# The set-up of an SSM's tables moved from beside the first FFN's down stage to beside its gate/up stage

## The chip, the cores and the metric

The kernel runs on one core of a Trainium2 chip. The metric is the device time of one execution in microseconds. The engines are named as in the profile: PE is TensorE (matmul), PEld its weight loads, DVE is VectorE, ACT is ScalarE, POOL is GpSimd, SP is SyncE. POOL, SP and ACT also issue DMAs.

## The reference, cut to what matters

One layer is computed for 1024 prompt tokens and 64 sample tokens together (1088 columns), all in float32:

```python
x = x + 0.5 * swiglu(rmsnorm(x), gate_a, up_a, down_a)      # first FFN: 1024 -> 2816 -> 1024
h = rmsnorm(x); q, k, v, u, g_attn, g_ssm = split(h @ w_in)
attn = windowed attention with sinks (q, k, v)
ssm  = glu(gelu(Re(C state_t) + D * u_t))                   # 32 groups, 64 states, 16 channels
x = x + (sigmoid(g_attn) * attn + sigmoid(g_ssm) * ssm) @ w_out
x = x + 0.5 * swiglu(rmsnorm(x), gate_b, up_b, down_b)      # second FFN, the same shapes
```

The SSM has a complex diagonal state per group: `abar = exp(lam * dt)`, `bbar = (abar - 1) / lam * b`, `h_t = abar * h_(t-1) + bbar * u_t`, `y_t = Re(c * h_t) + d * u_t`. The kernel evaluates it in chunks of eight tokens with tables that depend on the weights alone: powers of `abar` times `b` and `c`, the kernel of eight taps, and cosines and sines of the chunk's angle. Computing these tables is the set-up.

## The kernel before, in words

**Precision.** Every float32 operand of the large matmuls is split into a high part (rounded to fp32r by ACT) and a low part (the difference, by DVE), and each product is three matmuls.

**Stages of an FFN.** A start stage does two of 22 blocks of gate and up in the plain way. `g_stage` (L602) does the other 20, one unit each, by a Strassen scheme of seven products: per unit the steps P1, D (of the unit before), P6, P5, P27, each of several products of 12 matmuls, for two halves e of the columns. Weights come by SP's queue (L523), operands are split three steps ahead (`tasks`, L652 to L657), and the results are gathered by L705, L714, L721, L728 and L730; L732 writes the hidden block `hd` to DRAM from POOL's queue. Products X lie in PSUM banks of tags a and b (two buffers each), V and Y in tag d (three buffers). Then eight `d_unit`s (L779) read two or three hidden blocks and down weights back each, split them, and accumulate into x (L817), banks d and a. The first FFN's names end in a (psda, hida), the second's in b. The second FFN runs through the same `g_stage` and the same first seven `d_unit`s with nothing beside them.

**The side generator.** `run_units` runs the units' main generators one after another; each yield of a main is one tick (in `g_stage` one for six matmuls, 28 a unit, 560 in all; in a down unit of three blocks 36). `body` can attach a side generator: at each tick `rate` is added to an accumulator that starts at minus the lead, and for every full 1.0 the generator goes one step. The order of instructions on each engine is the order of these calls; the engines work in order, and waits between them are put in by the framework.

**The set-up** (`ssm_setup`, L897) is such a generator of 177 steps: loads of parameters on POOL's queue, some 24 steps on tiles of 128x32 (exponentials by a power on POOL, polynomials on DVE), and then eight blocks q of 19 steps on tiles of 128x512. A block transposes c (cT, L1072), makes S and C on DVE, transposes S (vl, L1092), forms k (L1100), makes C2 (L1110 to L1114), then the phases lo, ph, kk, kc (L1123 to L1136), the sines on ACT (L1138 to L1140), and writes each table to DRAM from POOL's queue (L1088 to L1147). The tables are read much later, in `ssm_core`. Small tiles come from a pool of five buffers (`s.sm`), large ones (weights, hidden blocks, operands, the parameter tile prm, ae, ssmin) from 43 buffers of one tag (`s.B`), PSUM banks by tag from `s.bank`: d 3, a 2, b 2, m 1. Before the change it is attached to `units[1]`, the first down unit, with rate 1.0 and lead 12.

Of the kernel before, what the change touches and what calls it, by code (L numbers as in the profile page):

```python
# [12 lines left out]
D = 1024  # L13
# [53 lines left out]
class Kern:  # L67
# [829 lines left out]
    def ssm_setup(s):  # L897
        nc, a = s.nc, s.a
# [2 lines left out]
        kpad = s.dr([16, NG, 256], "kpad")  # L901
        prm, ae, inp = s.B([128, 34, 32], "prm", F32), s.B([128, T], "ae", F32), s.B([128, 2, 512], "ssmin", F32)
        s.keep = s.small([128, 3, 32], "keep")
        free = list(range(34))

        def P():
            return prm[:, free.pop(0), :]
# [11 lines left out]
        def load_part(q):  # L919
            t = inp[:, q % 2, :]  # L920
            g0 = 4 * q
            for dst, hf, n in ((0, 0, "ssm_b_re"), (0, 1, "ssm_b_im"), (64, 0, "ssm_b_im"), (64, 1, "ssm_b_re")):
                nc.gpsimd.dma_start(t[hf * 64:(hf + 1) * 64, dst:dst + 64].rearrange("n (g c) -> n g c", g=4),
                                  a[n][0, g0:g0 + 4].rearrange("g n c -> n g c"))
            for dst, n in ((128, "ssm_c_re"), (192, "ssm_c_im"), (256, "ssm_c_im"), (320, "ssm_c_re")):
                nc.gpsimd.dma_start(t[0:64, dst:dst + 64], a[n][0, g0:g0 + 4].rearrange("g c n -> (g c) n"))
# [5 lines left out]
        for q in range(8):  # L932
            nc.gpsimd.dma_start(kpad[:, 4 * q:4 * q + 4, 0:128], z.rearrange("c (g x) -> c g x", g=4))
        yield
        ps = s.bank("b", "lamT")
        for i in range(2):
            nc.tensor.transpose(ps[:, i * 32:(i + 1) * 32], lam[:, i, :], s.id[:32, :32])
        lr, li, dt, mg, ang = P(), P(), P(), P(), P()
# [3 lines left out]
        e, c, p0 = P(), P(), P()  # L942
# [19 lines left out]
        def turns(x):  # L962

            k, kc, r = P(), P(), P()
            V.tensor_scalar(k, x, 1.0 / PI2, MAG, op0=OP.mult, op1=OP.add)
            V.tensor_scalar(kc, k, MAG, C14, op0=OP.subtract, op1=OP.mult)
            V.tensor_sub(r, x, kc)
            V.tensor_scalar(k, k, MAG, PI2 - C14, op0=OP.subtract, op1=OP.mult)
            return r, k

        r, k = turns(ang)
# [14 lines left out]
        V.scalar_tensor_tensor(sn, s2, 2.0, c2, op0=OP.mult, op1=OP.mult)  # L986
        V.tensor_mul(cs, s2, s2)
        yield
        t8, rhi, rlo = P(), P(), P()
        V.tensor_scalar(t8, ang, 8.0, None, op0=OP.mult)  # L990
        p8, q8 = turns(t8)
        yield
# [62 lines left out]
        V.tensor_scalar(AI, AI, -1.0, None, op0=OP.mult)  # L1055
        yield
        io = s.c1[:, C_IO:C_IO + 128]
        for q in range(8):
            g0 = 4 * q
            it = inp[:, q % 2, :]  # L1060
            gs = slice(g0, g0 + 4)

            def coef(x, lo, hi):
                n = hi - lo
                return x[:, lo:hi, gs].rearrange("p t g -> p g t").unsqueeze(3).to_broadcast([128, 4, n, 16])

            def chan(x, n):
                return x.rearrange("p (g c) -> p g c", g=4).unsqueeze(2).to_broadcast([128, 4, n, 16])

            pc = s.bank("b", f"cT{q}")  # L1070
            for i in range(2):
                nc.tensor.transpose(pc[:, i * 64:(i + 1) * 64], it[0:64, 128 + i * 128:256 + i * 128], s.id[:64, :64])  # L1072
            A.activation(it[:, 384:512], pc[:, 0:128], AF.Copy)
            bst, bsw, cc, csw = it[:, 0:64], it[:, 64:128], it[:, 384:448], it[:, 448:512]
            S, W = s.sm([128, 4, 8, 16], f"S{q}"), s.sm([128, 4, 8, 16], f"W{q}")
            V.tensor_mul(S, coef(ER, 0, 8), chan(bst, 8))
            yield
            V.tensor_mul(W, coef(EI, 0, 8), chan(bsw, 8))
            yield
            V.tensor_add(S, S, W)  # L1080
            yield
            C, W = s.sm([128, 4, 9, 16], f"C{q}"), s.sm([128, 4, 9, 16], f"W2{q}")
            V.tensor_mul(C, coef(AR, 0, 9), chan(cc, 9))
            yield
            V.tensor_mul(W, coef(AI, 0, 9), chan(csw, 9))
            yield
            V.tensor_add(C, C, W)
            nc.gpsimd.dma_start(s.tab1[gs, :, 192:320].rearrange("g p x -> p g x"), C[:, :, 1:9, :].rearrange("p g t c -> p g (t c)"))  # L1088
            yield
            pv = s.bank("b", f"vl{q}")  # L1090
            for g in range(4):
                nc.tensor.transpose(pv[:, g * 128:(g + 1) * 128], S[:, g].rearrange("p s c -> p (s c)"), s.id)  # L1092
            vl = s.sm([128, 4, 128], f"vls{q}")
            A.activation(vl, pv.rearrange("p (g x) -> p g x", g=4), AF.Copy)
            nc.gpsimd.dma_start(s.tab1[gs, :, 0:128].rearrange("g p x -> p g x"), vl)
            nc.gpsimd.dma_start(s.tab1[gs, :, 128:192].rearrange("g p x -> p g x"), vl[:, :, 0:64])
            yield
            pk = s.bank("b", f"k{q}")
            for g in range(4):
                nc.tensor.matmul(pk[:16, g * 128:(g + 1) * 128], S[:, g, 0, :], C[:, g, 0:8, :].rearrange("p t c -> p (t c)"), start=True, stop=True)  # L1100
            ks = s.sm([16, 4, 128], f"ks{q}")
            A.activation(ks, pk[:16].rearrange("p (g x) -> p g x", g=4), AF.Copy)
            dg = s.small([16, 4, 16], "dg", 2)
            V.tensor_mul(dg, s.id[0:16, 0:16].unsqueeze(1).to_broadcast([16, 4, 16]), dT[:, gs].unsqueeze(2).to_broadcast([16, 4, 16]))
            yield
            V.tensor_add(ks[:, :, 0:16], ks[:, :, 0:16], dg)
            nc.gpsimd.dma_start(kpad[:, gs, 128:256], ks)
            yield
            C2, W = s.sm([128, 4, 8, 16], f"D{q}"), s.sm([128, 4, 8, 16], f"W3{q}")
            V.tensor_mul(C2, coef(AI, 1, 9), chan(cc, 8))  # L1110
            yield
            V.tensor_mul(W, coef(AR, 1, 9), chan(csw, 8))
            yield
            V.tensor_sub(C2, C2, W)  # L1114
            nc.gpsimd.dma_start(s.tab2[gs, :, 0:128].rearrange("g p x -> p g x"), C2.rearrange("p g t c -> p g (t c)"))
            yield
            if q + 2 < 8:
                load_part(q + 2)
            ph, kk = s.sm([128, 4, 128], f"ph{q}"), s.sm([128, 4, 128], f"kk{q}")
            kc = s.sm([128, 4, 128], f"kc{q}")  # L1120
            iob = io.unsqueeze(1).to_broadcast([128, 4, 128])
            lo = s.sm([128, 4, 128], f"lo{q}")
            V.tensor_mul(ph, iob, rhi[:, gs].unsqueeze(2).to_broadcast([128, 4, 128]))  # L1123
            V.tensor_mul(lo, iob, rlo[:, gs].unsqueeze(2).to_broadcast([128, 4, 128]))
            yield
            V.tensor_add(kk, ph, lo)
            V.tensor_scalar(kk, kk, 1.0 / PI2, MAG, op0=OP.mult, op1=OP.add)
            yield
            V.tensor_scalar(kc, kk, MAG, C14, op0=OP.subtract, op1=OP.mult)
            V.tensor_scalar(kk, kk, MAG, PI2 - C14, op0=OP.subtract, op1=OP.mult)  # L1130
            yield
            V.tensor_sub(ph, ph, kc)
            V.tensor_sub(lo, lo, kk)
            yield
            V.tensor_add(ph, ph, lo)
            V.tensor_scalar(ph, ph, PIC, -PIC, op0=OP.min, op1=OP.max)  # L1136
            yield
            A.activation(kk, ph, AF.Sin, scale=0.5)  # L1138
            A.activation(kk, kk, AF.Square)
            A.activation(ph, ph, AF.Sin, scale=ns)  # L1140
            yield
            V.tensor_scalar(kk, kk, -2.0, 1.0, op0=OP.mult, op1=OP.add)
            nc.gpsimd.dma_start(s.tab3[gs, :, 0:128].rearrange("g p x -> p g x"), kk)
            nc.gpsimd.dma_start(s.tab3[gs, :, 128:256].rearrange("g p x -> p g x"), ph)
            yield
# [749 lines left out]
def at(u, before=None, after=None):  # L1895

    if before:
        main = u.main

        def run():  # L1900
            before()
            yield from main()
        u.main = run
    if after:
        u.end = after
    return u


def body(ctx, tc, a, o):
    s = Kern(ctx, tc, a, o)  # L1910
# [12 lines left out]
    def side(gen, rate, lead=0.0):  # L1923

        def f():
            s.drain_side()
            s.side, s.rate, s.acc = gen(), rate, -lead
            if lead:
                next(s.side)
        return f  # L1930

    units = s.ffn_units("a", ("f", 1))
    at(units[1], before=side(s.ssm_setup, 1.0, 12.0))

    def mix_begin():
        s.hready = 0
# [9 lines left out]
    q = [s.q_unit(f) for f in range(KC)]  # L1946
# [65 lines left out]
```

## Time and profile before

| | us |
|---|---|
| median of 3 runs (2352.77 to 2354.19) | 2353.74 |
| the profiled execution | 2351.03 |
| its span | 2349.3 |
| start, 0 to 90.4 | 90.4 |
| gate/up of the first FFN, 90.4 to 514.1 | 423.7 |
| down of the first FFN, units 1 to 7, 514.1 to 792.9 | 278.8 |
| down, unit 8 with the norm's sums, 792.9 to 831.8 | 38.9 |
| projections, attention, SSM, merge, start of the second FFN, 831.8 to 1645.6 | 813.8 |
| gate/up of the second FFN, 1645.6 to 2069.3 | 423.7 |
| down of the second FFN, units 1 to 7, 2069.3 to 2295.3 | 226.0 |
| last unit with the final norm, 2295.3 to 2349.3 | 54.0 |

The boundaries are read from the timeline of PE, by the tiles that its matmuls write. The windows view gives each engine's busy time between two times, the waits view who waited for whom. A matmul's length in the timeline overlaps the next one's; the distance between two starts is what it costs.

### The profile page before, as it was taken

The page shows a single profiled execution, that of the slowest core. Times are in us where ns is not written, and L with a number is a line of the kernel's source. Part 1 is how long each engine was busy: PE and PEld are TensorE (multiplying, and loading weights), DVE is VectorE, ACT ScalarE, POOL GpSimd, SP SyncE. Part 2 cuts the span into 40 slices and gives each one's busy share as a digit, 9 for nine tenths or more (in the row PEclk, how much of TensorE's full clock was granted, in tenths as well). Part 3 has the DMA queues.
Part 4 walks back from the last instruction along what each step waited for, and adds up shares of the span by engine and source line. Part 5 has one row for each costly group of instructions (what it writes and reads, how often), then busy time and mean ns, then how long its engine had stood idle before and what let it go on. Part 6 is the DMA issues. An engine that isn't in the chain of part 4 may idle for free. (4 is left out here: it accounts for less than half of the span.)

```text
span 2349.3 us, 39687 instructions
## 1 busy us (share of the span) xinstructions
PE 2275.0 (97%) x15910; PEld 2216.6 (94%) x15910; DVE 1404.2 (60%) x2961; ACT 853.0 (36%) x1919; POOL 264.3 (11%) x427
## 2 busy tenths in 40 slices
PE   7999999999889999999999999999999999999998
PEld 6999999998878998999998999989999999999997
DVE  7655555568888742446775666457555555575555
ACT  5333333331221341236666653223333333322113
POOL 2000000014333140002221100000000000000000
PEclk9999999999999999999999999999999999999999
DMA  6222222273443237740224164203222222362202
GB/s 197 79 73 83 83 75 64 83 255 108 140 138 106 73 131 215 238 107 28 69 75 111 45 231 136 73 5 140 79 83 66 73 83 83 126 256 72 86 10 77
DMA packets 234104, 250.04 MB, mean 106 GB/s; under 512 B 35056, under 2 KB 197024, under 8 KB 233888
## 3 DMA queue, kind: packets, MB, share of 16 engines
q1 hardware_dynamic: 218208, 205.42, 28.2%
q0 software_dynamic: 14272, 39.79, 4.8%
q8 instruction: 125, 2.05, 0.4%
q10 hardware_dynamic: 1440, 2.31, 0.3%
q14 instruction: 59, 0.48, 0.1%
HBM read 176.93 MB, written 74.60 MB: 107 GB/s over the span
## 5 line engine op out<-in xcount | busy, mean ns | idle before, releaser
L817 DVE SCALAR_TENSOR_TENSOR xr<-psdb,xr 128x384 f32<-128x384 f32 x168 | 87.9, 534 | 93.2 <-PE psdb L113 92.9
L817 DVE SCALAR_TENSOR_TENSOR xr<-psda,xr 128x384 f32<-128x384 f32 (+1 forms) x192 | 100.7, 532 | 33.5 <-PE psda L113 33.1
L1534 POOL TENSOR_SCALAR sm<-sm,sum 128x256 f32<-128x256 f32 x128 | 59.9, 487 | 312.3 <-DVE sum L1532 202.9
L113 PE MATMUL Ya<-b21h,a12a 128*128 128x272 f32 x320 | 67.1, 290 | 0.0
L113 PE MATMUL Xa<-t4h,a22a 128*128 128x272 f32 x320 | 67.1, 290 | 0.0
L113 PE MATMUL Yb<-b21h,a12b 128*128 128x272 f32 x320 | 67.1, 290 | 0.0
L113 PE MATMUL Xb<-t4h,a22b 128*128 128x272 f32 x320 | 67.1, 290 | 0.0
L113 PE MATMUL Vb<-b22h,s4b 128*128 128x272 f32 x320 | 67.1, 290 | 0.0
L113 PE MATMUL Va<-b22h,s4a 128*128 128x272 f32 x320 | 67.1, 290 | 0.0
L732 POOL DMA_DIRECT2D hd<-hidb x40 | 21.6, 540 | 403.0 <-DVE hidb L730 403.0
L732 POOL DMA_DIRECT2D hd<-hida x40 | 21.6, 540 | 403.0 <-DVE hida L730 403.0
L1518 ACT ACTIVATE sm<-sm,nm 128x256 f32<-128x256 f32 x128 | 63.3, 503 | 2.0 <-DVE nm L1505 1.9
L113 PE MATMUL Xa<-t2h,s2a 128*128 128x272 f32 x320 | 63.8, 290 | 0.0
L113 PE MATMUL Va<-t1h,s1a 128*128 128x272 f32 x320 | 63.8, 290 | 0.0
L113 PE MATMUL Xa<-t3h,s3a 128*128 128x272 f32 x320 | 63.8, 290 | 0.0
L113 PE MATMUL Xb<-t2h,s2b 128*128 128x272 f32 x320 | 63.8, 290 | 0.0
L113 PE MATMUL Xb<-t3h,s3b 128*128 128x272 f32 x320 | 63.8, 290 | 0.0
L113 PE MATMUL Vb<-t1h,s1b 128*128 128x272 f32 x320 | 63.8, 290 | 0.0
L113 PE MATMUL Xb<-b11h,a11b 128*128 128x272 f32 x320 | 63.8, 290 | 0.0
L113 PE MATMUL Xa<-b11h,a11a 128*128 128x272 f32 x320 | 63.8, 290 | 0.0
L104 ACT ACTIVATE hidhb<-rhidb 128x1088 fp32r<-128x1088 f32 x22 | 24.3, 1103 | 89.7 <-PE psdb L113 65.1
L113 PEld LDWEIGHTS Ya<-b21h,a12a 128*128 128x128 f32 x320 | 52.7, 188 | 0.0
(1455 smaller groups left out, 8498.9 us busy)
## 6 DMA issues: line engine op xcount, KB each, us to landing
xr<-xd SPq DMA_DIRECT2D x24, 544.0 KB, 6.0
rhida<-hd SPq DMA_DIRECT2D x22, 544.0 KB, 5.2
rhidb<-hd SPq DMA_DIRECT2D x22, 544.0 KB, 5.2
rdowna<-in_ffn_a_down_dram SPq DMA_DIRECT2D x22, 512.0 KB, 3.9
rdownb<-in_ffn_b_down_dram SPq DMA_DIRECT2D x22, 512.0 KB, 4.8
hd<-hida POOLq DMA_DIRECT2D x40, 272.0 KB, 2.9
hd<-hidb POOLq DMA_DIRECT2D x40, 272.0 KB, 2.7
rgatea<-in_ffn_a_gate_dram SPq DMA_DIRECT2D x20, 512.0 KB, 3.9
```

What stands on the lines that cost most here:

```text
L104: s.nc.scalar.activation(hi, raw, AF.Copy)
L113: s.nc.tensor.matmul(ps, w, x, start=i == 0 and not more, stop=i == n - 1, skip_group_check=more)
L732: nc.gpsimd.dma_start(s.hd[j, :, o:o + HC], hid[j][:, o:o + HC])
L817: nc.vector.scalar_tensor_tensor(xs, ps[:, :n], 0.5, xs, op0=OP.mult, op1=OP.add)
L1518: A.activation(sm[:, h, :], sm[:, h, :], AF.Exp, bias=nm[:, h:h + 1], accum_out=sm4[:, h:h + 1])
L1534: s.nc.gpsimd.tensor_scalar(sm[:, h, :], sm[:, h, :], sm4[:, h:h + 1], 1.0, op0=OP.mult, op1=OP.mult)
```

## The change

The set-up is attached to `units[0]`, the gate/up stage of the first FFN, with rate 0.36 in place of 1.0 and the same lead of 12. Its PSUM tiles come from tag m (one bank) in place of tag b. Six temporaries of a block (S and its W, C2 and its W, kc, lo) no longer come from the pool of five small buffers but lie in two slots of 16 rows of the parameter tile prm, whose first 32 rows hold no living value by then; rhi and rlo, which do live, move to rows 32 and 33.

```diff
--- before.py
+++ after.py
@@ -901,7 +901,7 @@
         kpad = s.dr([16, NG, 256], "kpad")
         prm, ae, inp = s.B([128, 34, 32], "prm", F32), s.B([128, T], "ae", F32), s.B([128, 2, 512], "ssmin", F32)
         s.keep = s.small([128, 3, 32], "keep")
-        free = list(range(34))
+        free = list(range(32))
 
         def P():
             return prm[:, free.pop(0), :]
@@ -932,7 +932,7 @@
         for q in range(8):
             nc.gpsimd.dma_start(kpad[:, 4 * q:4 * q + 4, 0:128], z.rearrange("c (g x) -> c g x", g=4))
         yield
-        ps = s.bank("b", "lamT")
+        ps = s.bank("m", "lamT")
         for i in range(2):
             nc.tensor.transpose(ps[:, i * 32:(i + 1) * 32], lam[:, i, :], s.id[:32, :32])
         lr, li, dt, mg, ang = P(), P(), P(), P(), P()
@@ -986,7 +986,7 @@
         V.scalar_tensor_tensor(sn, s2, 2.0, c2, op0=OP.mult, op1=OP.mult)
         V.tensor_mul(cs, s2, s2)
         yield
-        t8, rhi, rlo = P(), P(), P()
+        t8, rhi, rlo = P(), prm[:, 32, :], prm[:, 33, :]
         V.tensor_scalar(t8, ang, 8.0, None, op0=OP.mult)
         p8, q8 = turns(t8)
         yield
@@ -1055,6 +1055,10 @@
         V.tensor_scalar(AI, AI, -1.0, None, op0=OP.mult)
         yield
         io = s.c1[:, C_IO:C_IO + 128]
+
+        slot = [prm[:, 16 * i:16 * i + 16, :].rearrange("p a b -> p (a b)") for i in range(2)]
+        grid = [x.rearrange("p (g t c) -> p g t c", g=4, t=8) for x in slot]
+        flat = [x.rearrange("p (g x) -> p g x", g=4) for x in slot]
         for q in range(8):
             g0 = 4 * q
             it = inp[:, q % 2, :]
@@ -1067,12 +1071,12 @@
             def chan(x, n):
                 return x.rearrange("p (g c) -> p g c", g=4).unsqueeze(2).to_broadcast([128, 4, n, 16])
 
-            pc = s.bank("b", f"cT{q}")
+            pc = s.bank("m", f"cT{q}")
             for i in range(2):
                 nc.tensor.transpose(pc[:, i * 64:(i + 1) * 64], it[0:64, 128 + i * 128:256 + i * 128], s.id[:64, :64])
             A.activation(it[:, 384:512], pc[:, 0:128], AF.Copy)
             bst, bsw, cc, csw = it[:, 0:64], it[:, 64:128], it[:, 384:448], it[:, 448:512]
-            S, W = s.sm([128, 4, 8, 16], f"S{q}"), s.sm([128, 4, 8, 16], f"W{q}")
+            S, W = grid
             V.tensor_mul(S, coef(ER, 0, 8), chan(bst, 8))
             yield
             V.tensor_mul(W, coef(EI, 0, 8), chan(bsw, 8))
@@ -1087,7 +1091,7 @@
             V.tensor_add(C, C, W)
             nc.gpsimd.dma_start(s.tab1[gs, :, 192:320].rearrange("g p x -> p g x"), C[:, :, 1:9, :].rearrange("p g t c -> p g (t c)"))
             yield
-            pv = s.bank("b", f"vl{q}")
+            pv = s.bank("m", f"vl{q}")
             for g in range(4):
                 nc.tensor.transpose(pv[:, g * 128:(g + 1) * 128], S[:, g].rearrange("p s c -> p (s c)"), s.id)
             vl = s.sm([128, 4, 128], f"vls{q}")
@@ -1095,7 +1099,7 @@
             nc.gpsimd.dma_start(s.tab1[gs, :, 0:128].rearrange("g p x -> p g x"), vl)
             nc.gpsimd.dma_start(s.tab1[gs, :, 128:192].rearrange("g p x -> p g x"), vl[:, :, 0:64])
             yield
-            pk = s.bank("b", f"k{q}")
+            pk = s.bank("m", f"k{q}")
             for g in range(4):
                 nc.tensor.matmul(pk[:16, g * 128:(g + 1) * 128], S[:, g, 0, :], C[:, g, 0:8, :].rearrange("p t c -> p (t c)"), start=True, stop=True)
             ks = s.sm([16, 4, 128], f"ks{q}")
@@ -1106,7 +1110,7 @@
             V.tensor_add(ks[:, :, 0:16], ks[:, :, 0:16], dg)
             nc.gpsimd.dma_start(kpad[:, gs, 128:256], ks)
             yield
-            C2, W = s.sm([128, 4, 8, 16], f"D{q}"), s.sm([128, 4, 8, 16], f"W3{q}")
+            C2, W = grid
             V.tensor_mul(C2, coef(AI, 1, 9), chan(cc, 8))
             yield
             V.tensor_mul(W, coef(AR, 1, 9), chan(csw, 8))
@@ -1117,9 +1121,9 @@
             if q + 2 < 8:
                 load_part(q + 2)
             ph, kk = s.sm([128, 4, 128], f"ph{q}"), s.sm([128, 4, 128], f"kk{q}")
-            kc = s.sm([128, 4, 128], f"kc{q}")
+            kc = flat[1]
             iob = io.unsqueeze(1).to_broadcast([128, 4, 128])
-            lo = s.sm([128, 4, 128], f"lo{q}")
+            lo = flat[0]
             V.tensor_mul(ph, iob, rhi[:, gs].unsqueeze(2).to_broadcast([128, 4, 128]))
             V.tensor_mul(lo, iob, rlo[:, gs].unsqueeze(2).to_broadcast([128, 4, 128]))
             yield
@@ -1930,7 +1934,7 @@
         return f
 
     units = s.ffn_units("a", ("f", 1))
-    at(units[1], before=side(s.ssm_setup, 1.0, 12.0))
+    at(units[0], before=side(s.ssm_setup, 0.36, 12.0))
 
     def mix_begin():
         s.hready = 0
```

## Rows read from the trace of the kernel before

**Rows 1.** The page, section 1: busy time, share, instructions of each engine.

```profile
PE 2275.0 (97%) x15910; PEld 2216.6 (94%) x15910; DVE 1404.2 (60%) x2961; ACT 853.0 (36%) x1919; POOL 264.3 (11%) x427
```

**Rows 2.** Windows by stage: length, busy PE PEld DVE ACT POOL, PEclk, DMA.

```profile
90.40:514.10 423.70, 423.70 (x3363) 423.70 (x3362) 229.80 (x417) 155.09 (x341) 21.59 (x40) 1.00 0.29 92
514.10:792.90 278.80, 255.51 (x1486) 243.68 (x1485) 235.96 (x476) 66.03 (x89) 102.78 (x146) 0.96 0.43 136
1645.60:2069.30 423.70, 423.70 (x3362) 423.70 (x3361) 229.80 (x417) 154.86 (x341) 21.60 (x40) 1.00 0.29 93
2069.30:2295.30 226.00, 226.00 (x1371) 225.99 (x1370) 132.25 (x209) 40.78 (x41) 0.54 (x1) 1.00 0.25 89
```

**Rows 3.** Timeline of PE (start, us, what): the eighth down unit begins.

```profile
792.88 0.34 PE L113 MATMUL psda<-hidha,dna19h 128*128 128x384 f32 x1
```

**Rows 4.** Waits of PE, 514 to 832: us in total, times, longest.

```profile
PE vl L1092 <- DVE S L1080: 12.7, 5, 5.5
PE psda L113 <- DVE xr L817: 7.7, 6, 2.6
```

**Rows 5.** Windows of one three-block down unit in each FFN, columns as above.

```profile
584.40:631.30 46.90, 41.41 (x247) 39.61 (x246) 40.80 (x73) 12.48 (x19) 19.56 (x30) 0.96 0.45 138
2093.00:2128.70 35.70, 35.70 (x219) 35.70 (x218) 19.30 (x30) 4.49 (x5) 0.00 (x0) 1.00 0.23 76
```

**Rows 6.** Timeline of PE around L1092 (vl) and L1100 (k), one block.

```profile
626.51 0.34 PE L113 MATMUL psda<-hidla,dna7h 128*128 128x384 f32 x1
626.69 0.60 PE L1092 MATMUL vl<-c,S 128*128 128x128 f32 x4
627.04 0.42 PE L113 MATMUL psda<-hidha,dna7l 128*128 128x384 f32 x1
627.39 1.05 PE L1100 MATMUL k<-C,S 128*16 128x128 f32 x8
628.37 0.45 PE L113 MATMUL psda<-hidha,dna5h 128*128 128x384 f32 x1
628.65 0.34 PE L113 MATMUL psda<-hidla,dna5h 128*128 128x384 f32 x1
```

**Rows 7.** Line L1072, the transposes cT: duration ns min/median/max.

```profile
L1072 PE MATMUL cT<-c,ssmin x16: 222/247/273, 563.9 to 741.4; 64*128 64x64 f32 x16
```

**Rows 8.** Timeline of DVE in one gate/up unit (brackets: wait before).

```profile
203.62 0.69 DVE L657 TENSOR_TENSOR a22a<-rupa,a22a 128x512 fp32r<-128x512 f32 x1 [1.23 <-ACT a22a L652]
...
207.21 0.44 DVE L705 TENSOR_TENSOR hida<-hida,Ya 128x272 f32<-128x272 f32 x1 [0.24 <-PE Ya L113]
```

**Rows 9.** Timeline of PE where that unit's second Y product begins.

```profile
210.04 0.29 PE L113 MATMUL Ya<-b21h,a12a 128*128 128x272 f32 x1
```

**Rows 10.** Groups of DVE, 537 to 765: busy us, mean ns, idle before.

```profile
L1124 DVE TENSOR_TENSOR lo<-c,prm 128x512 f32<-128x512 f32 x8 | 5.5, 687 | 0.0
L1129 DVE TENSOR_SCALAR kc<-kk 128x512 f32<-128x512 f32 x8 | 3.7, 464 | 0.0
```

**Rows 11.** Line L1115, the write of C2 to DRAM from POOL's queue.

```profile
L1115 POOL DMA_DIRECT2D tab<-D x8: 764/764/767, 585.0 to 758.9; - x8
...
DMA to landing us min/median/max: 2.7/2.8/7.6
```

**Rows 12.** Groups of ACT, 514 to 792: the copy of vl.

```profile
L1094 ACT ACTIVATE vls<-vl 128x512 f32<-128x512 f32 x8 | 4.8, 598 | 44.5 <-PE vl L1092 38.6 <-DMA tab<-ph 5.9
```

**Rows 13.** Waits of ACT, 90 to 514.

```profile
ACT s2a L652 <- DVE rgatea L635: 55.0, 19, 2.9
```

**Rows 14.** Groups of ACT in the whole span: one of four table loads.

```profile
L1248 ACT ACT_TABLE_LOAD x1 | 1.3, 1283 | 0.0
```

**Rows 15.** Timeline of SP's DMA issues.

```profile
199.64 0.37 SPq L523 DMA_DIRECT2D rgatea<-in_ffn_a_gate_dram  x1
```

**Rows 16.** Timeline of ACT where those gate weights are first used.

```profile
221.64 0.62 ACT L652 ACTIVATE a11a<-rgatea 128x512 fp32r<-128x512 f32 x1
```

**Rows 17.** The page, section 6: issues, KB each, median us to landing.

```profile
rgatea<-in_ffn_a_gate_dram SPq DMA_DIRECT2D x20, 512.0 KB, 3.9
```

## The prediction

> **What bounds the kernel now.** I read the page's engine line first: PE is busy 97% of the span [rows 1], so only time in which PE waits, runs slowly or does extra work can be won. Next the windows by stage. The gate/up stage of the first FFN (90.4 to 514.1) and that of the second (1645.6 to 2069.3) take the same 423.7 us with PE busy throughout; neither has set-up work beside it [rows 2]. The down stage is different: its first seven units take 278.8 us in the first FFN, with the set-up, and the same seven take 226.0 in the second, without it [rows 2]. (The eighth unit starts with tile dna19h at 792.88 [rows 3]; it is followed by a normalisation in one FFN only, so I leave it out.) So the set-up costs 278.8 - 226.0 = **52.8 us** where it is.
>
> Where do these go? PE is idle 278.8 - 255.5 = 23.3 us; the granted clock is 0.96 on average instead of 1.00, which is some 11 us of work at the lower level [rows 2]; the rest is PE work of the set-up itself, counted below at 17.2. That sums to 51.7 of 52.8. The waits of PE name who is late: DVE, both for an eviction that frees a bank and for the set-up's own table S [rows 4]. The reason is one unit's DVE load: a three-block unit without set-up has 19.3 us of DVE work in 35.7; with set-up the unit at 584.4 holds 40.8 us of it and takes 46.9 [rows 5]. More than 35.7 doesn't fit, so DVE bounds the unit, and it keeps PE waiting.
>
> **The change part by part.** *Removed from the down stage*: all of the set-up, 235.96 - 132.25 = 103.7 us of DVE, 25.3 us of ACT, POOL's 102.8 us [rows 2]. What is late there next? Nothing that the second FFN's down stage shows: same units, DVE at 59%, PE busy 226.0 of 226.0. Gain 52.8 us in full.
>
> *Added to the gate/up stage: PE work.* This is paid in full, because PE has no idle time there. One of the eight table blocks of four groups: from the start of the matmul before the transposes (626.51) to the start of the second after the k products (628.65) pass 2.14 us; three ordinary matmuls lie in it, 0.18 apart elsewhere, so vl and k cost 1.60 [rows 6]. The two transposes cT are 0.247 each, 0.49 [rows 7]. 8 x 2.09 + 0.5 for the two transposes at the set-up's head (as cT) = **17.2 us**. A lower bound is the pitch of the instructions alone: 0.35 + 0.98 [rows 6] and one 0.25 for both cT, which overlap, times 8 = 12.6.
>
> *Added there: DVE work.* 229.8 + 103.7 = 333.5 us in a stage that becomes some 445 long: 75%, where the down unit above asked for over 100%. A step of the set-up is issued for every 1/0.36 = 2.8 ticks, and a tick is 423.7 / 560 = 0.757 us, so one step each 2.10 us. On average it fits; does it fit where DVE has a deadline? The tightest deadline that I find is a PSUM bank. The two Y products of a unit share one bank of tag d (V has the two others), so the second may start only when L705 has read the first. In the unit shown L705 starts at 207.21 and takes 0.44, and the second Y starts at 210.04 [rows 8, 9]: slack 2.4 us. In the 6.1 us before it DVE waits 1.23 and 0.24 us [rows 8], 1.47 that set-up steps may fill. In 6.1 us come 2.9 steps; three of the heaviest hold three tensor_tensors of 0.687 and three tensor_scalars of at most 0.464, 3.45 us [rows 10]. L705 is then 3.45 - 1.47 = 1.98 late, under 2.4: no PE wait from the arithmetic alone.
>
> *A new wait.* The temporaries C2 and lo now share one slot of the parameter tile. C2 goes to DRAM by POOL's queue, and lo may be written only when that write has read it. From the issue of C2's last step: 0.69 for its DVE operation, 0.76 on POOL, 2.8 (2.7 to 7.6) to landing [rows 10, 11] = 4.25; lo could begin one step and one operation later, 2.10 + 0.69 = 2.8. So DVE waits about 1.5 us in each block, 6.3 with the longest landing. Behind it on DVE stand the operand splits, which are made three steps ahead, and L705. The wait matters only if it falls in the stretch before L705, about 8 of 28 ticks, so in 2 or 3 of 8 blocks: 1.98 + 1.5 - 2.4 = 1.1 us each, **3 us** in sum; 0 if the heavy steps fall elsewhere, 3 x 5.9 = 18 with the longest landings.
>
> *Bank m.* The set-up had two banks b, now one bank m, so k's products wait until ACT has copied vl: 2.10 us between the steps, less 0.35 for the transposes and 0.60 for the copy, leaves 1.15 us [rows 6, 12]. ACT can be held by DVE for up to 2.9 us (s2 waits for the sums) [rows 13], which costs PE 1.75 us when vl falls behind it; that is 2.9 of a unit's 21.2 us, so about one block in eight: **1 us**, at most 8 x 1.75 = 14.
>
> *Edits at nothing.* ACT: 155.1 + 25.3 = 180 us of some 445 [rows 2], hidden under PE. Were the cover gone, each step would cost its copy, 0.6. POOL: 21.6 + 102.8 [rows 2]; its hd writes queue behind the set-up's loads, but they are read back only in the down stage. SP has no instruction of the set-up. The 177 steps end at tick (12 + 177) / 0.36 = 525 of 560, before the preparation of the down stage. Sine beside Silu: the trace has four table loads, none at L1138, although Silu ran before the first sine, so I take no switch [rows 14]. The Trainium skill ("ScalarE: Activation LUTs", What ACT_TABLE_LOAD costs) gives about 2.66 us for every switch to a different set; if sine needed another set than Silu, an estimate by that page is 16 switches, 43 us of ACT. The trace speaks against such a switch here.
>
> The sum, against the profiled execution: 2351.0 (span 2349.3 and 1.7 around it) - 52.8 + 17.2 + 4 = 2319.4. That execution lies 2.7 under the median of the runs, 2353.7, so **2322 us**.
>
> **Rivals.**
> *The shared slot bounds (slower).* Place: DVE at lo's first write. If the write of C2 landed late in every block, as the longest did (7.6), and each wait fell before an L705, PE would idle 8 x 5.9 = 47 us; the down stage shows 11 us of clock loss for 23.3 of idleness, a factor of 1.48, so 70 us. 2353.7 - 52.8 + 17.2 + 70 = 2388. It makes the kernel slower from about 3 us of PE idleness per block on (35.6 / 8 / 1.48), a wait of 3.4 us. For: the range of landings, and DVE works in order. Against: the median landing is 2.8, and blocks are 1.9 units long, so they meet L705 at different phases.
> *PE stalls on both small waits.* Bank m late in every block and the shared slot in three: 14 + 18, of which I take the half, 16, as a time to expect: 2353.7 - 52.8 + 17.2 + 16 = 2334, up to 2350.
> *Buffers.* Three of 43 large tiles are now held through the gate/up stage. SP already waits for free ones: the gate weights issued at 199.64 are first used at 221.64, 22.0 us later, 18.1 beyond their landing of 3.9 [rows 15 to 17]. A unit takes ten tiles in 21.2 us, so three fewer cost 6.4 of lead and leave 11.7. Were the lead gone, a wait of 1 us in each of 20 units would give 2342.
> *No gain.* The down stage's loss stays, or returns as the same 23.3 + 11 in the gate/up stage: 2322 - 4 + 34 = 2352. For: it is the same DVE work beside a PE that never rests. Against: 75% in place of over 100%.
> *Table switches.* If sine and Silu did evict each other when alternated, Silu would come 2 x 1.3 us late (the load's own row [rows 14]) in each block, before a DVE multiply that waits for it; 8 x 2.6 = 21 us: 2343.
> *The change doesn't do what it says.* If steps were left over for the down stage, each block there would still cost 52.8 / 8 = 6.6 and save 2.1 above, so 4.5 less gain per block; the count of steps speaks against it.
>
> **How the numbers follow.** Forecast (2314 to 2333) 0.72; PE stalls by the small waits (2333 to 2349) 0.13; buffers, table switches, steps left over (2333 to 2349) 0.04 together; no gain 0.05; the shared slot, slower, 0.04; under 2314 0.02. The low end is 2353.7 - 52.8 + 12.6 without a wait, 2314; the high end holds 22 us of PE stalls, 2340, over half of the two bounds of the small waits, 32. Outside lie 0.02 below and about 0.17 above. A measurement tells 0.2% (4.7 us) from no change: faster 0.91, same 0.05, slower 0.04.
>
> **What would show it.** The seven down units in 226 us with PE never idle and clock 1.00; the gate/up stage in 441 to 450 us, its PE idleness under 10; the waits of DVE with lo on the write of tab2 at about 1.5 us each; no wait of PE on DVE S; still four table loads. I am wrong if PE waits in the gate/up stage for L705 or for ACT's copy of vl by tens of us, or if the down stage keeps gaps without the set-up.

## The result and the profile after

The changed kernel takes **2325.44 us** (2321.59 to 2330.69, four runs) where the kernel before takes 2353.87 beside it: a ratio of 0.988, interval 0.986 to 0.990. The prediction was 2322, range 2314 to 2340. The profiled execution is the longest of the four, 2330.69 with a span of 2328.9; a second profile, below, has a span of 2324.3.

First the windows by stage of that first profile, which answer [rows 2]: length, busy time of PE, PEld, DVE, ACT, POOL, then PEclk and DMA. They are the gate/up stage of the first FFN, its first seven down units, the eighth, and everything up to the second FFN's gate/up stage.

```profile
89.69:541.57 451.88, 444.81 (x3476) 438.10 (x3475) 328.76 (x684) 175.99 (x389) 123.59 (x185) 0.99 0.39 123
541.57:767.52 225.95, 225.95 (x1371) 225.95 (x1369) 132.23 (x209) 40.66 (x41) 0.54 (x1) 1.00 0.28 96
767.52:806.47 38.95, 37.91 (x237) 37.48 (x236) 30.32 (x60) 18.08 (x34) 10.48 (x10) 1.00 0.05 15
806.47:1625.09 818.62, 795.05 (x5406) 762.48 (x5404) 450.83 (x1192) 352.56 (x914) 86.77 (x163) 0.98 0.38 115
```

The down units fell from 278.8 to 225.95, exactly what they take in the second FFN, with PE busy all the time at clock 1.00: the whole 52.8 us came. The gate/up stage grew from 423.7 to 451.9, by 28.2, of which PE's idle time is 451.88 - 444.81 = 7.1. The second FFN takes what it took. One line was not expected: the part between the two FFNs, 813.6 us before (813.8 in the table ahead, whose marks are rounder), became 818.6, though nothing is edited there; the second profile takes it up.

The waits of PE in the gate/up stage (who waited on what: us in total, times, longest) and the waits of DVE on a DMA there:

```profile
PE Ya L113 <- DVE hida L705: 6.1, 4, 2.6
PE k L1104 <- ACT vls L1098: 1.0, 1, 1.0
...
DVE prm L1128 <- DMA tab<-prm: 11.1, 8, 3.4
```

Line numbers are 4 higher than before: L1128 is lo's first write, L1119 the write of C2 to DRAM that it waits for. Eight blocks, eight waits, 1.4 us on average and from 0.2 to 3.4 each. In the timelines of DVE and PE one sees how such a wait reaches PE:

```profile
367.26 0.69 DVE L1128 TENSOR_TENSOR prm<-c,prm 128x512 f32<-128x512 f32 x1 [3.39 <-DMA tab<-prm]
367.87 0.68 DVE L657 TENSOR_TENSOR a22a<-rupa,a22a 128x512 fp32r<-128x512 f32 x1
...
372.19 0.43 DVE L705 TENSOR_TENSOR hida<-hida,Ya 128x272 f32<-128x272 f32 x1
...
369.77 0.29 PE L113 MATMUL Xa<-t3h,s3a 128*128 128x272 f32 x1
372.68 0.59 PE L113 MATMUL Ya<-b21h,a12a 128*128 128x272 f32 x1 [2.62 <-DVE hida L705]
373.07 0.43 PE L113 MATMUL Ya<-b21l,a12a 128*128 128x272 f32 x1
```

DVE stands 3.39 us before lo; behind it are queued the splits and sums of the gate/up stage and two more operations of the set-up (L1130, L1131), and then L705, which frees the bank for the second Y. PE idles 2.62 us, and then its matmuls follow each other at 0.39 and 0.22 in place of 0.13: the lower clock. The windows of 370 to 380 and 460 to 480 us, which hold two of these stalls, have granted clocks of 0.83 and 0.91:

```profile
370.00:380.00 10.00, 7.38 (x48) 7.33 (x48) 7.84 (x16) 5.17 (x12) 0.00 (x0) 0.83 0.17 50
460.00:480.00 20.00, 17.99 (x129) 17.40 (x129) 15.62 (x31) 7.19 (x16) 2.05 (x3) 0.91 0.34 104
```

ACT still loads four tables in all, none of them at the sines (L1142, L1144) although Silu now runs between them; the first stands at 1.2 us and the next at 908.8, so that none lies in the gate/up stage:

```profile
L140 ACT ACT_TABLE_LOAD x1 | 1.3, 1283 | 1.2 <-PEq L2003 1.2
L1252 ACT ACT_TABLE_LOAD x1 | 1.3, 1283 | 0.0
L1522 ACT ACT_TABLE_LOAD x1 | 1.3, 1283 | 0.0
L557 ACT ACT_TABLE_LOAD x1 | 1.3, 1283 | 0.0
```

### The profile page after: what moved, and what is told of

Read it like the earlier page. It is cut to its first block, busy times and chain, and to the rows that moved or that the text cites. A ratio compares the mean times of both kernels' runs of the same rounds, so it can differ in the third digit from the quotient of the medians.

```text
span 2328.9 us, 39773 instructions
## 1 busy us (share of the span) xinstructions
PE 2270.1 (97%) x15910; PEld 2216.7 (95%) x15910; DVE 1399.8 (60%) x2961; ACT 848.7 (36%) x1919; POOL 264.6 (11%) x427
## 3 DMA queue, kind: packets, MB, share of 16 engines
q1 hardware_dynamic: 218208, 205.42, 28.2%
q8 instruction: 125, 2.05, 0.4%
## 5 line engine op out<-in xcount | busy, mean ns | idle before, releaser
L732 POOL DMA_DIRECT2D hd<-hidb x40 | 21.7, 542 | 402.9 <-DVE hidb L730 402.9
L104 ACT ACTIVATE hidha<-rhida 128x1088 fp32r<-128x1088 f32 x22 | 24.3, 1103 | 116.7 <-PE psda L113 99.3
L156 POOL TENSOR_TENSOR rstd<-ms,mhalf 128x3 f32<-128x3 f32 x7 | 6.0, 859 | 477.4 <-DVE ms L504 477.4
```

Source lines behind the costliest of these rows:

```text
L104: s.nc.scalar.activation(hi, raw, AF.Copy)
L156: s.nc.gpsimd.tensor_tensor(r, ms, s.mhalf[:, 0:3], op=OP.pow)
L732: nc.gpsimd.dma_start(s.hd[j, :, o:o + HC], hid[j][:, o:o + HC])
```

## The experiments

My theory: the place brings the gain; in the gate/up stage the set-up pays its PE work, 17 us, and the rest of the 28 is stalls which the shared slot makes. Rivals: the stalls come from DVE's arithmetic whatever the slots are; DMAs or held tiles cost something; the layout or the bank carry part of the gain. Every time below is a median, with the interval of its ratio to the kernel before where it matters.

| kernel | us | gate/up stage | down units 1 to 7 |
|---|---|---|---|
| before | 2353.87 | 423.7 | 278.7 |
| changed | 2325.44 | 451.9 | 225.9 |
| changed, again | 2325.80 | 450.9 | 225.9 |
| lo and kc change slots | 2319.69 | 442.8 | 225.9 |
| temporaries in small buffers | 2317.70 | 442.8 | 225.9 |
| seven blocks: DMAs alone | 2303.21 | 427.7 | 225.9 |
| seven blocks: DMAs, PE and its copies | 2318.84 | 442.1 | 225.9 |
| down stage, new layout | 2374.62 | 423.7 | 300.9 |
| down stage, small buffers | 2353.58 | 423.7 | 279.7 |
| small buffers, rate 0.5 | 2337.15 | 462.5 | 225.9 |
| changed slots, rate 1.0 | 2404.43 | 526.3 | 225.9 |

**The same kernel again.** No edit.

> The changed kernel once more, nothing edited: its second profile is to tell which part of the first is the kernel's and which the execution's. In the first, the gate/up stage took 451.9 us (PE idle 7.1), the seven down units 226.0, and the part from the end of the down stage to the second FFN's gate/up stage 818.8, 5.0 more than in the kernel before although nothing is edited there. Theory A (the 5.0 us are the execution's): the middle part is back within 1.5 us of 813.8, the time is 2322 to 2326. Theory B (they are the change's: an order or a clock state that it leaves behind): 818 to 820 again, the time 2327 to 2331. By both: gate/up 449 to 453, down units 226.0.

2325.80 (2324.52 to 2326.15). The stalls are the kernel's: PE waits 6.4 us for L705, again in four places, and DVE 11.5 for the write of C2. The part between the FFNs took 815.2 us here. That is within the bound of theory A by a hair, and the other profiles speak for it: 817.4, 816.7, 815.4, 814.1, 815.0 and 818.4 with the set-up in the gate/up stage, 816.6 and 817.3 with it back in the down stage. The 813.6 of the kernel before is the lowest of these eleven values and the 818.6 of the first profile the highest. So the part varies by up to 5 us between executions, wherever the set-up is. Two things in it vary. Of the 5.0 us between the kernel before and the first profile, 2.5 are idle time of PE, most of it in one wait, before and after:

```profile
PE sy L1245 <- DVE p L1230: 3.2, 1, 3.2
PE sy L1249 <- DVE p L1234: 4.8, 1, 4.8
```

Most of the rest is clock: PE is busy at the lower level for 19.8 us there in the kernel before and for 24.7 in the first profile. Why the two vary wasn't found.

**lo and kc change slots.**

```diff
-            kc = flat[1]
+            kc = flat[0]
-            lo = flat[0]
+            lo = flat[1]
```

> lo and kc change places: lo is written into the slot that held W, kc into the one that held C2. Then lo waits for no write to DRAM, and kc, two steps (some 4.2 us) after lo, finds C2's write landed. Theory A (the shared slot makes the stalls): the waits of DVE on the write of tab2, 11.1 us in 8 times, vanish, PE's waits for L705 fall from 6.1 us to under 2, the gate/up stage from 451.9 to 444 to 447, the time 5 to 8 us under the changed kernel's, about 2318. Theory B (PE waits for L705 because of the set-up's arithmetic in DVE's queue, the wait merely stands in the same place): the waits on tab2 vanish, PE's waits for L705 stay at 4 to 7 us, the time within 2 us of the changed kernel's.

2319.69 (2319.15 to 2322.65), 6.1 us under the changed kernel on the same chip (2325.80, no overlap). No wait of DVE on the write of tab2 is left, nor one of kc, and PE's waits in the stage are these:

```profile
PE Ya L113 <- DVE hida L705: 1.2, 1, 1.2
PE k L1104 <- ACT vls L1098: 0.6, 1, 0.6
```

The window of its gate/up stage:

```profile
89.45:532.21 442.76, 440.92 (x3477) 435.26 (x3475) 328.20 (x684) 176.60 (x389) 123.70 (x185) 1.00 0.40 124
```

The same 328 us of DVE work are in it, and PE's idle time is 1.8 instead of 7.1. Theory A, and a little more than it asked: against the two profiles of the changed kernel the stage is 9.1 and 8.1 us shorter, where the idleness that went is 5.2 and 5.6.

**The temporaries back in the small buffers**, place, rate and bank as changed.

```diff
-            S, W = grid
+            S, W = s.sm([128, 4, 8, 16], f"S{q}"), s.sm([128, 4, 8, 16], f"W{q}")
...
-            C2, W = grid
+            C2, W = s.sm([128, 4, 8, 16], f"D{q}"), s.sm([128, 4, 8, 16], f"W3{q}")
...
-            kc = flat[1]
+            kc = s.sm([128, 4, 128], f"kc{q}")
...
-            lo = flat[0]
+            lo = s.sm([128, 4, 128], f"lo{q}")
```

> The changed kernel with S, W, C2, its W, kc and lo back in the pool of five small buffers, from which the gate/up stage takes its s1 as well; place, rate 0.36 and bank m stay. Theory A (the pool is enough at one step each 2.1 us; the layout into the parameters' tile is not what the gain needs): as with the swapped slots, 2318 to 2324, no wait on the write of tab2. Theory B (twelve tiles a block from five buffers, one of them held by s1, serialize steps and hold DVE, so that L705 and the splits come late): PE idle over 10 us in the gate/up stage, 2330 to 2360.

2317.70 (2315.77 to 2321.37), ratio 0.985, interval 0.984 to 0.987. That is theory A's, 0.3 under its range. The window of its gate/up stage:

```profile
89.64:532.41 442.77, 440.93 (x3477) 435.26 (x3475) 328.32 (x684) 176.42 (x389) 123.57 (x185) 1.00 0.40 125
```

It takes 442.77 us against 442.76 with the slots changed, with the same two waits of PE, 1.2 and 0.6. So the pool of five is enough at this rate, and the layout is no part of the gain; as written, with lo on C2's slot, it costs the stage 8 to 9 us.

**Seven of the eight blocks cut down to their DMAs.**

```diff
+            if q:
+                F, G = flat
...
+                nc.gpsimd.dma_start(s.tab2[gs, :, 0:128].rearrange("g p x -> p g x"), F)
+                yield
+                if q + 2 < 8:
+                    load_part(q + 2)
...
+                continue
```

> Seven of the eight table blocks are left out but for their DMAs: no transposes, products, DVE operations or ACT copies of blocks 1 to 7, and the tables written from whatever the slots hold. What is left is the floor of the place: the loads and writes on POOL's queue, the three large tiles held, and one block in full. Theory A (a block costs only PE work and the odd DVE stall; DMAs and held tiles cost nothing): gate/up stage 423.7 + about 2.7 + under 1 = 426 to 429 us, the time 24 us under the changed kernel's, 2299 to 2303. Theory B (DMAs or held tiles cost part of the 28.2 us that the stage grew by): gate/up stage 432 or more.

2303.21, and the gate/up stage 427.7. Theory A for the stage, with a time 0.2 over its range: 423.7 + 2.6 for the head and one block + the 1.2 of idleness that was measured is 427.5. DMAs on POOL's queue and the three large tiles held through the stage cost nothing that can be seen.

**The same seven blocks with their PE work and its copies.**

```diff
+                pc = s.bank("m", f"cT{q}")
+                for i in range(2):
+                    nc.tensor.transpose(pc[:, i * 64:(i + 1) * 64], it[0:64, 128 + i * 128:256 + i * 128], s.id[:64, :64])
...
+                for g in range(4):
+                    nc.tensor.transpose(pv[:, g * 128:(g + 1) * 128], F[:, g], s.id)
...
+                for g in range(4):
+                    nc.tensor.matmul(pk[:16, g * 128:(g + 1) * 128], F[:, g, 0:16], G[:, g], start=True, stop=True)
```

> As the kernel with the DMAs alone, but blocks 1 to 7 also do their transposes, products and ACT copies (left out of them: the DVE operations and the sines). Against that kernel it gives the price of PE work alone. Theory A (the prediction's 2.09 us a block): the gate/up stage 427.7 + 7 x 2.09 = 442.3 us, within 1.5; the time 2316 to 2319, and all that the changed kernel lies above it, 7 to 9 us, comes from DVE. Theory B (the price is the instructions' pitch, 1.58 a block, and the rest of the 28 us is stalls): 438 to 440, the time 2313 to 2315.

2318.84 (2315.31 to 2320.58). The windows of the gate/up stage of the kernel with the DMAs alone and of this one, in this order:

```profile
88.59:516.27 427.68, 426.46 (x3378) 425.40 (x3377) 254.81 (x530) 157.03 (x347) 122.96 (x185) 1.00 0.43 130
88.66:530.71 442.05, 440.81 (x3477) 435.22 (x3475) 254.91 (x530) 166.41 (x368) 122.84 (x185) 1.00 0.42 126
```

442.05 - 427.68 = 14.37, or 2.05 us a block; the prediction had 2.09. Read from starts in this trace, each block's cT takes 0.46, vl 0.44 and k 1.17. And 442.05 against 442.77 with all the DVE work: 73 us of DVE work cost PE 0.7 us, as long as nothing holds DVE up.

**Back to the down stage, with the new layout and bank m.**

```diff
-    at(units[0], before=side(s.ssm_setup, 0.36, 12.0))
+    at(units[1], before=side(s.ssm_setup, 1.0, 12.0))
```

> The set-up back beside the down stage (units[1], rate 1.0), with the changed kernel's bank m and its temporaries in the parameters' tile. Theory A (the place alone brings the gain): 2351 to 2358, the seven down units 277 to 284 us, PE waiting for DVE's xr and S. Theory B (the layout and the bank carry part of the gain, since five small buffers serialize the steps): under 2345, the down units under 270. At one step a tick of about 1.0 us lo comes 1.7 us after C2's issue, so the shared slot's wait should be about 2.5 us a block, 20 us of DVE in sum, and the time could reach 2365.

2374.62: 0.9% slower than the kernel before (interval 0.8 to 1.1%). The layout and the bank bring no gain by themselves, so theory B is out; but the time lies above theory A's range too, and above the 2365 that was its outer bound, and so do the down units. At one step a tick the shared slot is far worse. Waits of the stretch 512 to 815, which answer [rows 4]:

```profile
DVE prm L1128 <- DMA tab<-prm: 24.7, 8, 6.9
PE psda L113 <- DVE xr L817: 18.8, 11, 3.2
PE vl L1096 <- DVE prm L1084: 12.0, 6, 5.9
```

The wait on the write of tab2 is 3.1 us a block, which I had put at 2.5; PE's wait for xr rises from the 7.7 of [rows 4] to 18.8, and the units take 22.3 us more.

**Back to the down stage, with the small buffers**: both edits above together; against the kernel before only the bank differs and the list of parameter rows.

> Beside the down stage at rate 1.0, with the six temporaries in the small buffers: only bank m in place of bank b and the shorter list of parameter rows differ from the kernel before. With the shared slots in the same place the down units took 300.9 us, 22.2 more than the 278.7 of the kernel before. Theory A (the shared slots are the whole of these 22 us): 2351 to 2356, the down units 277 to 281. Theory B (bank m, whose k waits for ACT's copy of vl, is a part of it): the down units 285 or more, 2360 to 2375.

2353.58 (2349.06 to 2356.09), ratio 1.000, interval 0.999 to 1.001; the down units 279.7, theory A's:

```profile
513.11:792.85 279.74, 254.65 (x1484) 242.25 (x1483) 235.96 (x476) 66.02 (x89) 102.83 (x146) 0.96 0.43 135
```

So the shared slots are 21.2 of the 22.3 us. Bank m costs nothing that the times show; in the profile one wait of k for the copy of vl, 0.5 us, is its own. The set-up with bank b beside the gate/up stage wasn't tried.

Together with the small buffers beside the gate/up stage this leaves the place and the rate, which were moved together. A lower rate beside the down stage was not run. The first seven down units have 19 blocks and so 228 ticks, by the 36 of three blocks, and the set-up has to end before the eighth; 189 / 228 = 0.83 would be the lowest rate. The 235.96 us of DVE work there [rows 2] would then fill 97% of 226.0 + 17.2, an estimate that promises little by the run at rate 0.5 below.

**Rate 1.0 in the gate/up stage**, slots changed.

```diff
-    at(units[0], before=side(s.ssm_setup, 0.36, 12.0))
+    at(units[0], before=side(s.ssm_setup, 1.0, 12.0))
```

> The kernel with the swapped slots, at rate 1.0 in place of 0.36: the set-up, as dense as it was beside the down stage, now in the first third of the gate/up stage. A block holds 12 DVE operations of 0.685 us, three of 0.75 and five of 0.43, 12.6 us, and now comes every 19 ticks, so a unit of 28 ticks (21.2 us) holds 11.5 + 1.47 x 12.6 = 30.1 us of DVE work. Theory A (what decides is DVE work per time, and the rate is the working part of the change): DVE bounds for eight blocks, 5.4 units, and the loss is 5.4 x 8.9 = 48 us, with the clock's share up to 71: 2368 to 2390, slower than the kernel before. Theory B (the gate/up stage hides it in any density, the place is the working part): 2318 to 2326.

2404.43, 2.2% slower than the kernel before (interval 2.0 to 2.3%): the place gains nothing without the rate, as theory A has it. But its sum is too small, and the time lies above its range: the stage took 526.3 us, 84 more than at rate 0.36 where I expected 48 to 71. Two windows of the dense part and the longest waits of PE:

```profile
160.00:200.00 40.00, 30.13 (x194) 27.32 (x193) 29.82 (x56) 13.33 (x29) 16.28 (x26) 0.84 0.34 103
280.00:320.00 40.00, 28.80 (x203) 26.84 (x201) 31.38 (x60) 12.44 (x27) 13.19 (x20) 0.87 0.32 96
...
PE vl L1096 <- DVE prm L1084: 28.2, 7, 8.8
PE vl L1096 <- ACT s2a L652: 7.7, 1, 7.7
```

DVE is busy for 30 to 31 of 40 us and PE for 29 to 30: neither is full. PE stands before vl until DVE has made S, up to 8.8 us. DVE in its turn waits, from 120 to 320 us, 15.8 us in sum for PE's products and 24.4 for ACT, which itself waits for DVE; the largest of either kind:

```profile
DVE hida L714 <- PE Xa L113: 10.2, 4, 3.9
DVE hida L730 <- ACT ua L729: 7.1, 11, 1.9
```

The sum took DVE at 100%; engines that wait for each other in turn don't reach that. And not all is DVE's load: 13.5 of PE's 59.4 us of idleness are waits of vl and k that the profile puts down to ACT, which copies out what stands in the one bank m.

**Rate 0.5**, small buffers: the same line with 0.5.

> The kernel with the small buffers in the gate/up stage (place and bank m of the changed kernel), at rate 0.5 in place of 0.36: a block every 38 ticks, so a unit of 28 ticks holds 11.5 + 12.6 x 28 / 38 = 20.8 us of DVE work in 21.2, 98%, where rate 0.36 holds 18.2, 86%. At rate 1.0 (30.1 us asked for) the stage lost 100 us, though DVE was busy for only 30 of 40 us there: PE stood before vl, waiting for S. Theory A (only the average counts, and it still fits): gate/up stage 443 to 448 us, 2317 to 2323. Theory B (DVE that is full on average is late at every deadline in between, and PE waits for L705 and for S): PE idle 15 us or more in the first half of the stage, gate/up stage 465 to 500, 2340 to 2375.

2337.15 (2335.52 to 2340.84), the gate/up stage 462.5. PE's waits and the window of the stage:

```profile
PE Ya L113 <- DVE hida L705: 10.3, 6, 3.9
PE k L1104 <- ACT vls L1098: 4.3, 3, 1.9
PE k L1104 <- DVE C L1091: 0.6, 1, 0.6
...
88.80:551.26 462.46, 447.09 (x3477) 439.98 (x3475) 329.71 (x684) 176.81 (x389) 123.73 (x185) 0.99 0.39 121
```

Neither theory holds in full. PE's idleness is 462.46 - 447.09 = 15.4 us, but 8.8 of it in the first half of the stage, where B asked for 15; the stage and the time fall some 3 us short of B's ranges, and theory A, which asked for 448 at most, is further off. B's kind of wait, for L705, is the largest; 4.3 us are k's for the copy of vl, which is bank m's wait. An average of 98% fits on paper and costs 19.7 us against 86%. Both percentages are sums of durations; in the windows of 330 to 370 us, rate 0.36 first and rate 0.5 second, the durations add up to 32.6 and 37.5 us, but DVE is busy for 29.6 and 33.7 of 40, since its operations overlap a little, and PE goes from 40.0 to 37.4:

```profile
330.00:370.00 40.00, 40.00 (x317) 39.35 (x316) 29.59 (x58) 16.86 (x37) 12.01 (x19) 1.00 0.41 119
330.00:370.00 40.00, 37.44 (x294) 36.50 (x293) 33.65 (x65) 15.70 (x37) 12.14 (x19) 1.00 0.41 121
```

## Why the prediction was right

- **The down stage, -52.8.** Measured 278.66 - 225.95 = 52.7, PE never idle. Nothing new was late there, as the second FFN had shown.
- **PE work, +17.2.** With the DVE work of seven blocks left out, the stage less its idle time is 440.81, 17.1 over the 423.73 without set-up. The step of reading a block's price from starts before and after it held: 2.05 against 2.09, and vl and k 1.61 against 1.60. The sum of the durations in [rows 6, 7], 2.14, would have served nearly as well here. The lower bound (12.6, from the pitch alone) would have been wrong.
- **DVE's arithmetic, no wait of PE.** Right for the blocks: 0.7 us for the DVE work of seven. One wait of 1.2 us for L705 is there even without that work, at 168 us, in the set-up's head. There two steps in a row hold six operations each (L1038 to L1043; from 160.40 to 165.58 they take 4.0 us of DVE), more than the three heaviest of a block that I had reckoned with, 3.45 us.
- **The shared slot, +3.** The mechanism was right and so was the mean wait, 1.4 us a block where 1.5 was forecast, but the size of what PE loses was not: the two slots changed, the stage is 9.1 and 8.1 us shorter than in the two profiles of the changed kernel. Two things were mis-sized. I priced the meeting of wait and L705 with the mean wait, 1.1 us in each of 2 or 3 blocks; PE lost 2.6 and 2.0 us in two, after waits of 3.39 and 2.15, and 0.2 in a third. And I charged the clock only in the rivals, at 1.48 us for each us of idleness, not in the forecast. Here 5.2 us of idleness cost 9.1 in one profile, and 5.6 cost 8.1 in the other.
- **Bank m, +1.** One wait of k for the copy of vl, 1.0 us; 0.6 with the slots changed.
- **Edits at nothing.** POOL's DMAs and the held tiles: 427.5 by the sum against 427.7 in the kernel with the DMAs alone. ACT's copies: no wait of PE for them in the kernel that adds them and PE's work. Four table loads, as the rows of before made likely. An estimate by the Trainium skill's figure ("ScalarE: Activation LUTs", What ACT_TABLE_LOAD costs) was 43 us of ACT if sine needed another set than Silu; the trace shows no such switch. The page's 2.66 us are about 1.28 for the load and about 1.38 for a drain. The trace agrees with the first, 1.283 us, and shows nothing of the second: the load at 1032.01 us begins 0.02 us after the activation before it ends, and the next activation begins at 1033.30.
- **The sum.** Forecast for the profiled execution 2319.4, second profile 2326.1 (span 2324.3 and 1.8 around it). The difference of 6.7 is 6.0 in the gate/up stage (450.9 against 444.9), 1.6 between the FFNs and -1.0 in the start. In the medians the error is 3.4, in part because of the correction of 2.7 from the profiled execution of before to its median: that execution had the shortest part between the FFNs. That the number came out closer than the stage is luck, made in parts in which nothing is edited.

Of the rivals, "PE stalls on both small waits" (2334) was right in its half on the slot, three blocks, and not in its half on bank m, one wait in place of eight; beyond PE's work the stage lost 10.1 to 11.1 us, where this rival had 16. "The shared slot bounds" didn't come at rate 0.36; in the down stage at rate 1.0 the slots did cost, 21 to 22 us.

## What to carry to other kernels

Work moved beside a saturated engine costs that engine's own share of it and little else, provided that the other engines keep room: here, with no slot in the way, a rate that gave DVE work of 86% of its time was nearly free, one of 98% cost 20 us and one of 142% cost 84 (sums of durations; waits at the one bank m are in these costs). When temporaries are laid into shared memory, order them so that none takes the place of one that a DMA is still reading; two names exchanged were worth 8 to 9 us of the stage. The version with the old buffers, 2317.70, and the one with the names exchanged, 2319.69, are the fastest that do all the work; their runs overlap and don't tell them apart. A wait is priced by the cases that meet a deadline, here 3.39 and 2.15 us, and by what the clock adds, not by its mean.

## What the runs showed of the hardware

The time lost was always more than PE's idle time, by a factor of 1.36 to 1.56. Taking 17.1 us for the set-up's PE work, the stage that holds the set-up lost beyond that work:

| kernel, stage | PE idle | lost in sum | factor | PE busy at the lower clock |
|---|---|---|---|---|
| changed, gate/up | 7.1 | 451.9 - 423.7 - 17.1 = 11.1 | 1.56 | 6.5 |
| changed, again, gate/up | 7.4 | 450.9 - 423.7 - 17.1 = 10.1 | 1.36 | 3.4 |
| rate 0.5, gate/up | 15.4 | 462.5 - 423.7 - 17.1 = 21.7 | 1.41 | 10.2 |
| rate 1.0, gate/up | 59.4 | 526.3 - 423.7 - 17.1 = 85.5 | 1.44 | 52.3 |
| before, down | 23.3 | 278.7 - 225.9 - 17.1 = 35.7 | 1.53 | 20.5 |
| new layout, down | 37.8 | 300.9 - 225.9 - 17.1 = 57.9 | 1.53 | 33.2 |
| small buffers, down | 25.1 | 279.7 - 225.9 - 17.1 = 36.7 | 1.46 | 17.4 |

The last column is PE's busy time in the stretches in which the trace has the lower level (1.2 GHz) granted; the gate/up stages with 1.8 us of idleness or less have none. Around the stall of 2.62 us shown above, matmuls of 272 columns start 0.126 us apart before it (368.76 to 369.77) and 0.226 after it (373.07 to 374.65), so at the lower level 44% of the time is lost. That accounts for between a half and nine tenths of what was lost beyond idleness; the rest isn't placed.

The same stall doesn't always cost the clock. L705 holds PE for 2.01 us before 466.40 in the first profile of the changed kernel and for 2.01 before 466.66 in the second. In the first the lower level follows (0.91 in the window of 460 to 480 above, with 129 matmuls), in the second it doesn't:

```profile
460.00:480.00 20.00, 17.99 (x141) 17.55 (x141) 15.89 (x31) 7.27 (x17) 2.05 (x3) 1.00 0.35 107
```

The 3.1 us less at the lower level, by 44% some 1.4 us, and 0.3 more of idleness make about the 1.0 us between the two gate/up stages, 451.9 and 450.9.
